# Two layers of a hybrid backbone on one core: the second FFN's input kept whole, its convolution in seven parts, and on-chip memory laid out anew

## The chip, the core and the metric

The kernel runs on one core of a Trainium2 chip. A core has five engines with queues of their own: TensorE (PE) for matrix products, VectorE (DVE), ScalarE (ACT) and GpSimd (POOL) for elementwise work, and SyncE (SP), which here only issues transfers. Transfers go over 16 DMA engines. The metric is the device time of one execution in microseconds; the median of three runs is quoted.

## The reference

Two layers, each a token mixer and a gated convolutional feed-forward network (FFN), on 1024 latent and 128 context tokens of width 1024 (`D_FF` is 2816):

```python
def _pre(x, m, g, j):
    return rmsnorm(x, g) * (1 + m[:, 3 * j + 1, None]) + m[:, 3 * j, None]

def _post(x, y, m, g, j):
    return x + m[:, 3 * j + 2, None] * rmsnorm(y, g)

def conv_ffn(h, w_up, cw, cb, w_down):
    u = dwconv(h @ w_up, cw, 1) + cb
    g, val = jnp.split(u, 2, axis=-1)
    return (jax.nn.gelu(g) * val) @ w_down

# for each layer l:
        xp = _post(xp, yp, m_p, norm_g[l, 1], 0)     # yp, ys: the mixer, with its output product @ w_out
        xs = _post(xs, ys, m_s, norm_g[l, 1], 0)
        xp = _post(xp, conv_ffn(_pre(xp, m_p, norm_g[l, 2], 1), *ffw), m_p, norm_g[l, 3], 1)
        xs = _post(xs, conv_ffn(_pre(xs, m_s, norm_g[l, 2], 1), *ffw), m_s, norm_g[l, 3], 1)
```

Layer 0's mixer is a state-space scan beside differential attention, layer 1's a short gated convolution beside a linear recurrence. All is fp32.

## The kernel before

The 1152 tokens are nine tiles of 128. Each fp32 product is made of three products of halves (`mm3`, L115): every operand is split into `hi` (a copy by ACT to a shorter fp32 format) and `lo` (the rest, a subtraction on DVE or POOL).

The stages follow one another: layer 0's mixer (to about 790 us), the first output stage (`mixer_out(0)`, L1343, to 1000), the first FFN (`ffn`, to 1840), layer 1's mixer (to 2166), the second output stage (`mixer_out(1)`, to 2267), the second FFN's up product (`up`, L1530, to 2838), its down product (`down2`, L1611, to 3139) and a tail.

**An output stage** goes over the nine tiles. For tile t, SP loads `yr` (mixer output) and `x` (residual), in layer 0 also `rb` (row scales, L1353); DVE multiplies `yr` by `rb` (L1365, layer 0 only), ACT makes `yh` (L1367), DVE `yl` (L1368), and PE runs 48 products into the tiles `ops`. `post` (ACT L289, POOL L175 and L178, DVE L303 and L304) normalizes them and adds `x`, which SP stores (L1378); `pre` (ACT L289, POOL, DVE L311) normalizes again, PE transposes (`tps`, L317), ACT applies scale and shift (`h`, L320), DVE casts (`hh`, L322) and POOL makes `hl` (L323). Both `rb` and `h` come from the pool `cv`. The order of an engine's instructions, and the slots of a pool, are set by the framework's scheduler from the program, so a tile of a pool's memory that is free late moves work in every queue.

**The second up product** forms 128 rows of both halves of `w_up` as a 2x2 block product (the 1152 tokens in two halves of `HT` = 576), with seven products in place of eight. A product (`prod`, L1489) is 24 matmuls of 128x288 into `sps`, so a block of 128 channels has 168, and there are 22 blocks (`NFB`). The input's blocks are 11, 12, 21 and 22 (512 channels by 576 tokens), and four sums of them, T1 to T4, are needed. Before, the blocks are kept as hi and lo alone; `forms` (L1500) adds them back (`whole`, L1509), makes the sums and splits these, after the first products of two blocks. Weight sums and splits are made per product (`pair`, L1478). `up_rest` (L1584) is the convolution: per half one ACT and four DVE operations over 1152 tokens, then gelu, a product and a split, and two stores of `m` per block. `down2` loads `m` back by tiles (`mt`) and the weights `wd`, and runs 1188 products `dps`.

```python
        bs = [block(fb) for fb in range(NFB)]
        next(bs[0])
        next(bs[1])
        F.extend(self.forms(H))
```

Of the kernel before, what the change touches and what calls it, by code (L numbers as in the profile page):

```python
# [39 lines left out]
class Whole:  # L40
# [9 lines left out]
class Blocks:  # L50


    def __init__(self, k):
        self.b = {x: [k.big.tile([128, 4, HT], F32R, tag="big", name=k.nm("h" + s)) for s in "hl"]
                  for x in ((0, 0), (1, 0), (1, 1), (0, 1))}

    def parts(self, q, c0, c1):
        out = []
        for n in range(2):
            a, b = max(c0, n * HT), min(c1, n * HT + HT)  # L60
            if a < b:
                out.append((a - c0, b - c0, [x[:, :, a - n * HT:b - n * HT] for x in self.b[q, n]]))
        return out
# [24 lines left out]
class K:  # L88
    def __init__(self, tc, a, o, ctx):
        self.tc, self.nc, self.a, self.o = tc, tc.nc, a, o  # L90
        self.P = lambda name, bufs, **kw: tc.tile_pool(name=name, bufs=bufs, **kw)
        self.dram = {}
        self.lastw, self.wdma = None, []
        P = lambda name, bufs, **kw: ctx.enter_context(self.P(name, bufs, **kw))
        self.dr = P("dr", 1, space=DRAM)
# [210 lines left out]
    def pre(self, t, x, tmp, cols, H):  # L306
# [5 lines left out]
        for q in range(2):  # L312
            ps = self.pt.tile([128, 4, 128], F32, tag="pt", name=self.nm("tps"))
            h = self.cv.tile([128, 4, 128], F32, tag="cv", name=self.nm("h"))
# [3 lines left out]
            for i in range(4):  # L318
                b = q * 4 + i
                nc.scalar.activation(h[:, i], ps[:, i], AF.Identity, scale=sc[:, b:b + 1], bias=sh[:, b:b + 1])  # L320
            for o0, o1, (hv, lv) in H.parts(q, t * 128, t * 128 + 128):
                nc.vector.tensor_copy(hv, h[:, :, o0:o1])  # L322
                nc.gpsimd.tensor_tensor(lv, h[:, :, o0:o1], f(hv), op=OP.subtract)  # L323
# [1019 lines left out]
    def mixer_out(self, l, W, xin, xout, H, keep={}):  # L1343
# [142 lines left out]
    def bank2(self, name):  # L1486
        return self.ps.tile([128, 2, 512], F32, tag="ps", name=self.nm(name))

    def prod(self, p, y):  # L1489

        nc = self.nc
        ps = self.bank2("sps")
        w = HT // 2
        steps = [(p[:, x, k], y[j][:, k]) for k in range(4) for x, j in ((0, 0), (0, 1), (1, 0))]
        for n, (x, y) in enumerate(steps):
            for c in range(2):
                nc.tensor.matmul(ps[:, c, :w], x, y[:, c * w:c * w + w], start=n == 0, stop=n == len(steps) - 1)  # L1497
        return ps[:, :, :w]

    def forms(self, H):  # L1500

        nc = self.nc
        V, G = nc.vector, nc.gpsimd
        T2, T1, T4 = ([self.big2.tile([128, 4, HT], F32R, tag="big2", name=self.nm(n + s)) for s in "hl"] for n in ("T2", "T1", "T4"))
        T3 = H.b[0, 1]

        def whole(out, q, n, k, eng):
            h, l = H.b[q, n]
            eng.tensor_tensor(out, f(h[:, k]), f(l[:, k]), op=OP.add)  # L1509

        def put(t, k, src, eng):
            nc.scalar.activation(t[0][:, k], src, AF.Copy)
            eng.tensor_tensor(t[1][:, k], src, f(t[0][:, k]), op=OP.subtract)
        for k in range(4):
            A, B, C = (self.mid_tile([128, 2, HT], "tf") for _ in range(3))
            whole(C[:, 0], 0, 1, k, V)
            whole(A[:, 0], 0, 0, k, G)
            whole(A[:, 1], 1, 1, k, V)
            V.tensor_tensor(A[:, 0], C[:, 0], A[:, 0], op=OP.subtract)
            V.tensor_tensor(B[:, 0], A[:, 1], A[:, 0], op=OP.subtract)  # L1520
            put(T2, k, B[:, 0], V)
            put(T1, k, A[:, 0], V)
            whole(B[:, 1], 1, 0, k, G)
            V.tensor_tensor(A[:, 1], A[:, 1], C[:, 0], op=OP.subtract)
            put(T3, k, A[:, 1], G)
            V.tensor_tensor(B[:, 1], B[:, 0], B[:, 1], op=OP.subtract)
            put(T4, k, B[:, 1], G)
        return T1, T2, T3, T4

# [389 lines left out]
```

## Time and profile before

| | |
|---|---|
| median of three runs | 3152.21 us (3146.33 to 3155.35) |
| the profiled execution | 3149.71 us, its span 3147.8 us |
| mean granted clock of PE | 0.941 |
| busy PE / DVE / POOL / ACT | 2822.0 / 2057.8 / 1250.4 / 1156.5 us |

Times in the rows below are microseconds from the start of the span. The busy share of PE is high over the whole span, so the places to read are the stages where it is not: there the chain of waits and the timeline say what PE waits for. The granted clock is given as a share of full speed.

### The profile page before, as it was taken

The numbers are of one execution on the slowest core, as the hardware profiler recorded it, in microseconds if no ns is written. First come the engines' busy times: TensorE is split into PE (matmuls) and PEld (weight loads), VectorE is DVE, ScalarE is ACT, GpSimd is POOL, SyncE is SP. The second block draws the span as 40 slices with busy tenths as digits, with TensorE's granted clock in tenths as the row PEclk, the third lists the DMA queues.
The fourth block names the chain that finished last, engine by engine and source line by source line (L and its number), as shares of the span: only waits on it lengthen the run. The fifth ranks groups of instructions, "written<-read, shape, count | busy, mean of one in ns | idle before, by whom it ended". The sixth has DMA issues, their size and how long they took to land.

```text
span 3147.8 us, 42033 instructions
## 1 busy us (share of the span) xinstructions
PE 2822.0 (90%) x15724; PEld 2536.6 (81%) x15724; DVE 2057.8 (65%) x3321; ACT 1156.5 (37%) x1946; POOL 1250.4 (40%) x1263
## 2 busy tenths in 40 slices
PE   7877888888667999999999989999879999997998
PEld 4875666777456999999999969998679999996887
DVE  6777767997323988888755686546468777773113
ACT  5221115675223322222222265555434444443101
POOL 3699954774111000000000161112467777764222
PEclk8988889998778999999999989999979999998999
DMA  6425457345222333333211232123302222229555
GB/s 212 141 82 138 109 148 200 85 106 168 88 70 72 98 91 98 89 97 97 73 41 41 67 126 76 51 84 128 121 14 101 93 93 101 93 79 249 134 105 154
DMA packets 357738, 331.46 MB, mean 105 GB/s; under 512 B 47134, under 2 KB 312050, under 8 KB 357534
## 3 DMA queue, kind: packets, MB, share of 16 engines
q1 hardware_dynamic: 273656, 264.47, 26.7%
q0 software_dynamic: 66464, 49.16, 7.3%
q10 hardware_dynamic: 17414, 15.14, 1.7%
q8 instruction: 124, 2.03, 0.3%
q14 instruction: 80, 0.66, 0.1%
HBM read 246.54 MB, written 82.16 MB: 104 GB/s over the span
## 4 chain that ended last, share of the span: by engine, by line
PE 51%; DVE 6%; POOL 5%; issue 3%; DMA 2%; ACT 2%; ACTq 0%; POOLq 0%; DVEq 0%; SPq 0%
PE pps L121 23%; PE dps L1635 8%; PE sps L1497 8%; PE dps L121 7%; PE ops L121 3%; DVE cc L1598 1%; POOL C L1536 1%; POOL ws L1536 1%; DMA wv<-ffn_w_up 1%; PE gps L121 1%; POOL wv L1536 1%; DMA mw<-w_mod 1%; ACT cc L1594 1%; POOL wp L1483 0%; DVE C L1536 0%
## 5 line engine op out<-in xcount | busy, mean ns | idle before, releaser
L121 PE MATMUL pps<-hh,whi 128*128 128x384 f32 (+1 forms) x1824 | 625.3, 343 | 1.0 <-ACT whi L131 0.5
L121 PE MATMUL pps<-hh,wlo 128*128 128x384 f32 (+1 forms) x1824 | 623.5, 342 | 2.2 <-DVE wlo L133 2.2
L121 PE MATMUL pps<-hl,whi 128*128 128x384 f32 (+1 forms) x1824 | 623.7, 342 | 0.4 <-POOL hl L831 0.4
L121 PEld LDWEIGHTS pps<-hh,whi 128*128 128x128 f32 x1824 | 349.6, 192 | 11.9 <-issue 3.2
L121 PEld LDWEIGHTS pps<-hh,wlo 128*128 128x128 f32 x1824 | 349.3, 192 | 8.4 <-DVE wlo L133 3.2
L121 PEld LDWEIGHTS pps<-hl,whi 128*128 128x128 f32 x1824 | 349.7, 192 | 4.5 <-POOL hl L831 0.7
L133 POOL TENSOR_TENSOR wlo<-wr,whi 128x1024 fp32r<-128x1024 f32 x22 | 55.1, 2510 | 740.0 <-PE dps L121 595.8
L1635 PE MATMUL dps<-wp,mt 128*128 128x512 f32 x1188 | 280.2, 398 | 20.3 <-ACT wp L1482 20.3
L1635 PEld LDWEIGHTS dps<-wp,mt 128*128 128x128 f32 x1188 | 225.2, 190 | 75.1 <-issue 20.5
L1497 PE MATMUL sps<-hh,wp 128*128 128x288 f32 x1408 | 257.5, 300 | 10.5 <-DVE wp L1483 2.5
L1497 PEld LDWEIGHTS sps<-hh,wp 128*128 128x128 f32 x1408 | 213.9, 192 | 12.8 <-issue 4.8
L1406 DVE SCALAR_TENSOR_TENSOR cc<-pps,cvc,cc 128x384 f32<-128x384 f32 (+2 forms) x352 | 171.0, 509 | 37.3 <-ACT cc L1403 35.1
L265 DVE SCALAR_TENSOR_TENSOR macc<-mw,sil,macc 128x256 f32<-128x256 f32 x392 | 175.6, 482 | 22.3 <-DMA mw<-w_mod 22.0
L1598 DVE SCALAR_TENSOR_TENSOR cc<-C,cvc,cc 128x1023 f32<-128x1023 f32 (+1 forms) x176 | 173.4, 1034 | 21.0 <-ACT cc L1594 21.0
L131 ACT ACTIVATE whi<-wr 128x1024 fp32r<-128x1024 f32 x102 | 107.6, 1057 | 164.7 <-PE pps L121 98.6
L1452 DVE TENSOR_TENSOR acc<-acc,dps 128x512 f32<-128x512 f32 x180 | 122.2, 680 | 68.8 <-PE dps L121 68.0
L1137 POOL TENSOR_TENSOR wl<-wf,wh 128x512 fp32r<-128x512 f32 (+2 forms) x96 | 144.4, 1523 | 50.6 <-DVE ra L1107 41.7
L121 PE MATMUL dps<-whi,mh 128*128 128x512 f32 x396 | 155.9, 394 | 2.3 <-DVE acc L1452 2.3
L121 PE MATMUL dps<-wlo,mh 128*128 128x512 f32 x396 | 155.3, 392 | 0.0
L121 PE MATMUL dps<-whi,ml 128*128 128x512 f32 x396 | 154.9, 391 | 0.0
L1403 ACT ACTIVATE cc<-pps,cvc 128x385 f32<-128x385 f32 (+1 forms) x132 | 87.5, 665 | 179.5 <-PE pps L121 154.0
L1497 PE MATMUL sps<-hl,wp 128*128 128x288 f32 x704 | 153.0, 299 | 0.0
(425 smaller groups left out, 6334.1 us busy)
## 6 DMA issues: line engine op xcount, KB each, us to landing
mw<-w_mod SPq DMA_DIRECT2D x224, 128.0 KB
m<-cc SPq DMA_DIRECT2D x44, 576.0 KB
x<-x SPq DMA_DIRECT2D x45, 512.0 KB
wr<-ffn_w_up SPq DMA_DIRECT2D x44, 512.0 KB
wm<-w_mod SPq DMA_DIRECT2D x40, 512.0 KB
mt<-m POOLq DMA_DIRECT2D x36, 448.0 KB, 4.7
k<-kh POOLq DMA_DIRECT2D x8, 1408.0 KB, 6.4
wr<-ffn_w_down SPq DMA_DIRECT2D x22, 512.0 KB
```

The lines of the kernel that those rows point to most:

```text
L121: nc.tensor.matmul(ps, x, y, start=first and i == 0 and j == 0, stop=last and i == n - 1 and j == 2)
L131: nc.scalar.activation(hi, raw, AF.Copy)
L133: (eng or nc.vector).tensor_tensor(lo, raw, f(hi), op=OP.subtract)
L265: nc.vector.scalar_tensor_tensor(acc[v], wt, s, acc[v], op0=OP.mult, op1=OP.add)
L1137: pin((nc.vector if late else nc.gpsimd).tensor_tensor(vl, u.wf[b][:, :k], f(vh), op=OP.subtract))
L1403: nc.scalar.activation(cc[:, :no], ps[:, q:q + no], AF.Identity, bias=cw[3], scale=cw[1])
L1406: nc.vector.scalar_tensor_tensor(cc[:, oa - o0:ob - o0], ps[:, oa + d - i0:ob + d - i0], cw[j], cc[:, oa - o0:ob - o0], op0=OP.mult, op1=O ...
L1452: nc.vector.tensor_tensor(acc[t][:, sl], acc[t][:, sl], ps, op=OP.add)
L1497: nc.tensor.matmul(ps[:, c, :w], x, y[:, c * w:c * w + w], start=n == 0, stop=n == len(steps) - 1)
L1536: tt = lambda e, o, x, y, op: e.tensor_tensor(o, x, y, op=op)
L1598: nc.vector.scalar_tensor_tensor(cc[:, o0:o1], src[:, o0 + d:o1 + d], cw[j], cc[:, o0:o1], op0=OP.mult, op1=OP.add)
L1635: nc.tensor.matmul(ps[:, h], mt[:, x, i], W[fb][:, y, h * 512:h * 512 + 512], start=i == 0 and j == 0, stop=i == n - 1 and j == 2)
```

## The change

**The input kept whole.** `Blocks` keeps the four blocks of the second FFN's input as plain fp32. T1 and T2 are formed and split in the second output stage itself, tile by tile, for the tiles of the second half (`put`). A new function `rest` splits 11, 22 and 21 and forms and splits T3 and T4; it takes 20 ACT copies, 24 DVE and 8 POOL operations of 128x576.

**The up product** is one list of products: the first product of block n+1 stands ahead of the last of block n, weights are split two products ahead, and the convolution is a generator whose seven parts stand between the next products. Its last subtraction goes from DVE to POOL; of the seven evictions DVE has five (before four), ACT two.

**Memory.** Pools wait by the tile that overlaps and not by the whole pool that was closed (`reuse_waits`); the pools of `layers` are opened in another order; `rb` has a pool of its own with one buffer; the block buffers close ahead of the last product (`early`), which then loads four weights and two tiles' rows of the down product. That product takes its first two tiles together.

```diff
@@ class Blocks: the second FFN's input
+        self.raw, self.lo, self.hi = {}, {}, {}
+        self.raw["11"] = new("r11", "b11", F32)
+        for x in ("T1", "T2"):
+            self.lo[x], self.hi[x] = new(x + "l", x + "l"), new(x + "h", x + "h")
+        for x in ("12", "22", "21"):
+            self.raw[x] = new("r" + x, "b" + x, F32)
...
+        if t * 128 + 128 > HT and q:
+            cs = slice(max(t * 128 - HT, 0), t * 128 + 128 - HT)
+            R = lambda x: self.raw[x][:, :, cs]
+            t1, t2 = (k.cv.tile([128, 4, 128], F32, tag="cv", name=k.nm("t"))[:, :, :cs.stop - cs.start] for _ in range(2))
+            V.tensor_tensor(t1, R("12"), R("11"), op=OP.subtract)
+            V.tensor_tensor(t2, R("22"), t1, op=OP.subtract)
+            for x, s, e in (("T2", t2, V), ("T1", t1, G)):
+                h, l = self.hi[x][:, :, cs], self.lo[x][:, :, cs]
+                A.activation(h, s, AF.Copy)
+                e.tensor_tensor(l, s, f(h), op=OP.subtract)
...
+        def split(x, src, e):
+            for i in range(4):
+                A.activation(self.hi[x][:, i], src[i], AF.Copy)
+                e.tensor_tensor(self.lo[x][:, i], src[i], f(self.hi[x][:, i]), op=OP.subtract)
+        raw = {x: [r[:, i] for i in range(4)] for x, r in self.raw.items()}
+        temp = lambda: [t[:, i] for t in [k.mid.tile([128, 2, HT], F32, tag="cc", bufs=4, name=k.nm("tf")) for _ in range(2)] for i in range(2)]
+        self.hi["11"], self.lo["11"] = new("h11"), new("l11")
+        split("11", raw["11"], V)
+        t3 = temp()
+        for i in range(4):
+            G.tensor_tensor(t3[i], raw["22"][i], raw["12"][i], op=OP.subtract)
+        self.hi["22"], self.lo["22"] = new("h22"), new("l22", "r12")
+        split("22", raw["22"], V)
+        t4 = temp()
+        for i in range(4):
+            V.tensor_tensor(t4[i], raw["21"][i], f(self.hi["T2"][:, i]), op=OP.subtract)
+        self.hi["21"], self.lo["21"] = new("h21", "r22"), new("l21", "r11")
+        split("21", raw["21"], G)
+        self.hi["T3"], self.lo["T3"] = new("T3h"), new("T3l")
+        split("T3", t3, V)
+        for i in range(4):
+            V.tensor_tensor(t4[i], t4[i], f(self.lo["T2"][:, i]), op=OP.subtract)
+        self.hi["T4"], self.lo["T4"] = new("T4h"), new("T4l")
+        split("T4", t4, V)
@@ K.__init__
-        self.P = lambda name, bufs, **kw: tc.tile_pool(name=name, bufs=bufs, **kw)
+        self.P = lambda name, bufs, **kw: tc.tile_pool(name=name, bufs=bufs, **({} if kw.get("space") == DRAM else {"reuse_waits": "tile"}), **kw)
@@ mixer_out
-                rb = self.cv.tile([128, 4, 128], F32, tag="cv", name=self.nm("rb"))
+                rb = self.rsb.tile([128, 4, 128], F32, tag="rb", name=self.nm("rb"))
@@ up
-        bs = [block(fb) for fb in range(NFB)]
-        next(bs[0])
-        next(bs[1])
-        F.extend(self.forms(H))
-        for fb in range(NFB):
-            next(bs[fb])
-            if fb > 0 and fb + 1 < NFB:
-                next(bs[fb + 1])
+        PRODS = (("S2", "T2", G), ("S1", "T1", V), ("11", "11", V), ("S4", "22", G), ("12", "21", V), ("S3", "T3", V), ("22", "T4", V))
+        def split(n, i):
+
+            u = fbs[n]
+            if i == 0:
+                u.s = wt("s", 1)
+                w = u.w = {"11": u.g[:, 0:4], "12": u.g[:, 4:8], "21": u.v[:, 0:4], "22": u.v[:, 4:8], "S1": u.s[:, 0:4], "S2": u.s[:, 4:8]}
+                tt(G, w["S1"], w["21"], w["22"], OP.add)
+                tt(G, w["S2"], w["S1"], w["11"], OP.subtract)
+            u.p[i] = self.pair(u.w[PRODS[i][0]], PRODS[i][2], self.wr, "p", 3)
+            if i == 1:
+                w = u.w
+                w["S4"], w["S3"] = w["S2"], w["21"]
+                tt(G, w["S4"], w["12"], w["S2"], OP.subtract)
+                tt(G, w["S3"], w["11"], w["21"], OP.subtract)
...
+        order = [(0, i) for i in range(6)]
+        for n in range(1, NFB):
+            order += [(n, 0), (n - 1, 6)] + [(n, i) for i in range(1, 6)]
+        order.append((NFB - 1, 6))
+        for u in fbs:
+            u.p, u.bank = {}, {}
+        load(0)
+        load(1)
+        split(0, 0)
+        split(0, 1)
+        rests = []
+        for m, (n, i) in enumerate(order):
+            if m + 2 < len(order):
+                split(*order[m + 2])
+            prod(n, i)
+            if m == 0:
+                H.rest(self)
+            if i == 5:
+                rests.append(self.up_rest(l, n, fbs[n].C))
+            if rests and next(rests[0], 1):
+                rests.pop(0)
+            evict(n, i)
+            if i == 6 and n + 2 < NFB:
+                load(n + 2)
+            if m == len(order) - 2:
+                early()
@@ up_rest
-        nc.vector.tensor_tensor(m, m, h, op=OP.subtract)
+        nc.gpsimd.tensor_tensor(m, m, h, op=OP.subtract)
@@ down2, layers
+            for ts in ((0, 1),) + tuple((t,) for t in range(2, NT)) if gi == 0 else tuple((t,) for t in range(NT)):
...
+            with self.P("rsb", 1) as self.rsb:
+                self.mixer_out(0, W, self.xsrc, x1, Whole(hh, hl))
...
+        def early():
+            bctx.close()
+            R = lambda name, bufs: rctx.enter_context(self.P(name, bufs, side="right"))
+            self.wrd, self.wd0, self.dm = R("wrd", 4), R("wd0", 4), R("dm", 3)
+            self.Wd = {}
+            for i in range(4):
+                self.down_w(1, i)
+                if i < 2:
+                    rows[0, i] = self.down_rows(1, 0, i)
```

The change moves instructions in every queue. Three places follow; a name ends in the program's number of the tile.

**First output stage, SP's loads and stores** (`rb`, `yr` and `x` of a tile have consecutive even numbers; the stores go to `x_7965` before and `x_7959` after). Before:

```order
L1358 DMA yr_8118<-y_5319 128x8x128
L1360 DMA x_8120<-x_sample 128x1024
L1378 DMA x_7965<-x_8014 128x1024
L1353 DMA rb_8116<-rs 128x4x128
L1358 DMA yr_8224<-y_5319 128x8x128
L1360 DMA x_8226<-x_sample 128x1024
L1378 DMA x_7965<-x_8120 128x1024
L1353 DMA rb_8222<-rs 128x4x128
```

After:

```order
L1405 DMA yr_8124<-y_5313 128x8x128
L1407 DMA x_8126<-x_sample 128x1024
L1400 DMA rb_8228<-rs 128x4x128
L1405 DMA yr_8230<-y_5313 128x8x128
L1407 DMA x_8232<-x_sample 128x1024
L1425 DMA x_7959<-x_8020 128x1024
L1400 DMA rb_8334<-rs 128x4x128
L1405 DMA yr_8336<-y_5313 128x8x128
L1407 DMA x_8338<-x_sample 128x1024
L1400 DMA rb_8440<-rs 128x4x128
```

Before, the store of tile 0 (`x_8014`) stands ahead of `rb` of tile 1 and of the loads of tile 2; now `rb`, `yr` and `x` of tile 2 stand ahead of the store of tile 0 (`x_8020`), and all loads of tile 3 with `rb` of tile 4 ahead of the store of tile 1.

**The same place on DVE**: L1365 and L1412 are the scaling by `rb`, L1368 and L1415 make `yl`, L304 and L357 add the residual, L322 and L53 cast `h`. Before:

```order
L304 SCALAR_TENSOR_TENSOR x_8014<-tmp_8071,rs,x_8014 128x1024
L311 TENSOR_SCALAR tmp_8071<-x_8014,q 128x1024
L322 CAST hh_7992<-h_8093 128x4x128
L1365 SCALAR_TENSOR_TENSOR yr_8118<-yr_8118,dag,rb_8116 128x512
L322 CAST hh_7992<-h_8105 128x4x128
L1368 TENSOR_TENSOR yl_8123<-yr_8118,yh_8122 128x1024
L303 TENSOR_TENSOR tmp_8177<-ops_8127,tab__1423_7994 128x512
L292 TENSOR_TENSOR s_8181<-ss 128x1
```

After:

```order
L1415 TENSOR_TENSOR yl_8129<-yr_8124,yh_8128 128x1024
L345 TENSOR_TENSOR s_8081<-ss 128x1
L356 TENSOR_TENSOR tmp_8077<-ops_8028,tab__1423_8000 128x512
L357 SCALAR_TENSOR_TENSOR x_8020<-tmp_8077,rs,x_8020 128x1024
L1412 SCALAR_TENSOR_TENSOR yr_8230<-yr_8230,dag,rb_8228 128x512
L364 TENSOR_SCALAR tmp_8077<-x_8020,q 128x1024
L356 TENSOR_TENSOR tmp_8183<-ops_8133,tab__1423_8000 128x512
L1415 TENSOR_TENSOR yl_8235<-yr_8230,yh_8234 128x1024
L53 CAST hh_7995<-h_8103 128x4x128
L53 CAST hh_7995<-h_8115 128x4x128
L345 TENSOR_TENSOR s_8187<-ss 128x1
```

The scaling of the next tile stood behind the cast of this tile's `h`; now the scaling of the tile after the next stands ahead of this tile's L364 and its cast.

**End of the second output stage on ACT**: `h` (before) and `b` (after) are scale and shift, `wp` the first weight pairs, L99 and L88 the copies of `rest` and `put`. Before:

```order
L289 ACTIVATE junk,ss<-ops_20254 128x512
L320 ACTIVATE h_20222<-tps_20221,mc_19408,mc_19402 128x128 x4
L320 ACTIVATE h_20234<-tps_20233,mc_19408,mc_19402 128x128 x4
L289 ACTIVATE tmp_20303,ssq<-x_20247 128x1024
L1482 ACTIVATE wp_20381<-wg_20372 128x512
L1482 ACTIVATE wp_20411<-wg_20372 128x512
L1482 ACTIVATE wp_20441<-wg_20372 128x512
L320 ACTIVATE h_20325<-tps_20324,mc_19408,mc_19402 128x128 x4
L320 ACTIVATE h_20337<-tps_20336,mc_19408,mc_19402 128x128 x4
```

After:

```order
L78 ACTIVATE b_3000_19398<-tps_20319,mc_19415,mc_19409 128x128 x4
L78 ACTIVATE b_3001_19399<-tps_20328,mc_19415,mc_19409 128x128 x4
L99 ACTIVATE h_3109_20417<-b_2995_19393 128x576 x4
L88 ACTIVATE T1h_19395<-t_20337 128x4x128
L99 ACTIVATE h_3113_20433<-b_3001_19399 128x576 x4
L88 ACTIVATE T2h_19397<-t_20338 128x4x128
L99 ACTIVATE T3h_20459<-tf_20427 128x576 x2
L99 ACTIVATE T3h_20459<-tf_20428 128x576 x2
L99 ACTIVATE h_3117_20449<-b_3002_19400 128x576 x4
L99 ACTIVATE T4h_20473<-tf_20443 128x576 x2
L99 ACTIVATE T4h_20473<-tf_20444 128x576 x2
L1522 ACTIVATE wp_20381<-ws_20378 128x512
```

Three weight pairs stood ahead of the last tile's `h`; now all copies of `rest` stand ahead of the first weight pair.

**End of the up product on SP**: `m` are the convolution's stores, `wd` and `wr` the down weights. Before:

```order
L1607 DMA m_20787<-cc_25414 128x1152
L1607 DMA m_20787<-cc_25421 128x1152
L1620 DMA wd_25689<-ffn_w_down 128x1024
L1620 DMA wd_25694<-ffn_w_down 128x1024
L1620 DMA wd_25699<-ffn_w_down 128x1024
L1620 DMA wd_25704<-ffn_w_down 128x1024
L1607 DMA m_20787<-cc_25651 128x1152
L1607 DMA m_20787<-cc_25658 128x1152
L1620 DMA wd_25709<-ffn_w_down 128x1024
```

After:

```order
L1669 DMA m_20840<-cc_25618 128x1152
L1669 DMA m_20840<-cc_25629 128x1152
L1678 DMA wr_25550<-ffn_w_down 128x1024
L1678 DMA wr_25558<-ffn_w_down 128x1024
L1678 DMA wr_25566<-ffn_w_down 128x1024
L1678 DMA wr_25571<-ffn_w_down 128x1024
L1669 DMA m_20840<-cc_25636 128x1152
L1678 DMA wr_25678<-ffn_w_down 128x1024
L1678 DMA wr_25683<-ffn_w_down 128x1024
```

The first four weights stood behind both stores of block 20 (`cc_25414`, `cc_25421`); now they stand ahead of the second of these (`cc_25636`).

## Rows read from the trace of the kernel before

**Rows 1.** The page: busy time of PE; the second down product's group.

```profile
PE 2822.0 (90%) x15724; PEld 2536.6 (81%) x15724; DVE 2057.8 (65%) x3321; ACT 1156.5 (37%) x1946; POOL 1250.4 (40%) x1263
...
L1635 PE MATMUL dps<-wp,mt 128*128 128x512 f32 x1188 | 280.2, 398 | 20.3 <-ACT wp L1482 20.3
```

**Rows 2.** Busy time, 80 us of the first output stage: PE, PEld, DVE, ACT, POOL, PEclk, DMA.

```profile
880.00:960.00 80.00, 47.68 (x176) 37.65 (x176) 21.96 (x29) 21.64 (x51) 15.44 (x20) 0.74 0.28 84
```

**Rows 3.** Timeline, one tile of the first output stage: start, length, engine, line.

```profile
851.55 0.39 PE L121 MATMUL ops<-Wo,yl 128*128 128x512 f32 x1
...
855.48 0.43 SPq L1353 DMA_DIRECT2D rb<-rs  x1
...
858.00 1.97 PE L317 MATMUL tps<-misc,tmp 128*128 128x128 f32 x8 [6.07 <-DVE tmp L311]
...
859.22 2.90 ACT L320 ACTIVATE h<-tps,mc,mc 128x128 f32<-128x128 f32 x8 [2.96 <-PE tps L317]
...
861.21 1.85 DVE L1365 SCALAR_TENSOR_TENSOR yr<-yr,dag,rb 128x512 f32<-128x512 f32 x1
...
864.26 2.07 PE L121 MATMUL ops<-wo,yh 128*128 128x512 f32 x4 [4.29 <-ACT yh L1367]
```

**Rows 4.** Busy time, a whole tile of each output stage, columns as in 2.

```profile
888.10:913.00 24.90, 14.68 (x56) 11.65 (x56) 7.20 (x10) 6.35 (x15) 5.51 (x7) 0.77 0.25 74
2197.50:2209.20 11.70, 11.70 (x57) 9.78 (x56) 5.14 (x9) 6.22 (x16) 4.14 (x6) 1.00 0.37 134
```

**Rows 5.** Chain of waits, second output stage: start, length, what.

```profile
2185.68 10.90 PE ops L121 x48
2196.59 0.87 PE tps L317 x8
...
2256.32 10.91 PE ops L121 x48
```

**Rows 6.** Timeline, last product of the first output stage's first tile.

```profile
801.75 0.39 PE L121 MATMUL ops<-Wo,yl 128*128 128x512 f32 x1
```

**Rows 7.** Chain of waits, last tile of the first output stage.

```profile
986.83 12.87 PE ops L121 x48
```

**Rows 8.** Chain of waits, from the second output stage to the first up products.

```profile
2279.32 0.51 POOL q L178
...
2285.94 18.48 PE sps L1497 x120
```

**Rows 9.** Busy time in the stall after them, columns as in 2.

```profile
2305.00:2345.00 40.00, 24.75 (x92) 19.41 (x90) 39.65 (x32) 11.71 (x19) 29.96 (x17) 0.62 0.00 0
```

**Rows 10.** Groups by line and shape, 2305 to 2353 us: times, busy, mean ns.

```profile
L1509 POOL TENSOR_TENSOR tf<-hh,hl 128x576 f32<-128x576 f32 x8 | 15.0, 1874 | 6.9 <-DVE tf L1524 6.1 <-DVE T1l L1513 0.8
L1509 DVE TENSOR_TENSOR tf<-hh,hl 128x576 f32<-128x576 f32 x8 | 11.9, 1492 | 0.0
...
L1524 DVE TENSOR_TENSOR tf<-tf,tf 128x576 f32<-128x576 f32 x4 | 3.0, 746 | 0.0
...
L1512 ACT ACTIVATE T2h<-tf 128x576 fp32r<-128x576 f32 x4 | 2.7, 680 | 2.6 <-DVE tf L1520 2.6
```

**Rows 11.** Chain of waits, steady part of the second up stage.

```profile
2566.67 22.64 PE sps L1497 x168
...
2590.18 22.64 PE sps L1497 x168
```

**Rows 12.** Timeline, from the last up products to the down product.

```profile
2835.15 2.34 SPq L1620 DMA_DIRECT2D wd<-ffn_w_down  x4
...
2835.51 1.43 POOL L1536 TENSOR_TENSOR C<-X,Y 128x576 f32<-128x576 f32 x1 [10.18 <-issue]
...
2837.61 0.42 PE L1497 MATMUL sps<-T4h,wp 128*128 128x288 f32 x2
```

**Rows 13.** Chain of waits, the same stretch.

```profile
2850.62 6.40 DMA m<-cc
...
2858.32 26.79 PE dps L1635 x102
```

More of the change, by code (lines that the diff above doesn't have):

```diff
@@ L50 @@
 class Blocks:
     def __init__(self, k):
[L54 to L58, printed above, removed]
-        for n in range(2):
[L60 to L63, printed above, removed]
+        new = lambda tag, n, dt=F32R: k.big.tile([128, 4, HT], dt, tag=tag, name=k.nm(n))
@@ new lines, in rest @@
+    def rest(self, k):
+        nc = k.nc
+        V, G, A = nc.vector, nc.gpsimd, nc.scalar
+        new = lambda n, tag=None: (k.big if tag else k.big2).tile([128, 4, HT], F32R, tag=tag or "big2", name=k.nm(n))
+        def split(x, src, e):
[18 more added lines that the diff above has]
+        split("T3", t3, V)
+        for i in range(4):
+            V.tensor_tensor(t4[i], t4[i], f(self.lo["T2"][:, i]), op=OP.subtract)
+        self.hi["T4"], self.lo["T4"] = new("T4h"), new("T4l")
+        split("T4", t4, V)
@@ L317, in pre @@
                 nc.tensor.transpose(ps[:, i], tmp[:, b * 128:(b + 1) * 128], self.id)
[L318 to L323, printed above, removed]
+            H.put(self, t, q, ps, sc, sh)
     def xsrc(self, t):
@@ L1484, in pair, with up @@
         return p
[L1486 to L1528, printed above, removed]
-    def up(self, l, H):
+    def up(self, l, H, early):
         nc = self.nc
@@ new lines, in prod, with evict @@
+        def prod(n, i):
+            u = fbs[n]
+            x = PRODS[i][1]
+            ps = u.bank[i] = self.bank2("sps")
+            y = H[x]
+            steps = [(u.p[i][:, w, k], y[j][:, k]) for k in range(4) for w, j in ((0, 0), (0, 1), (1, 0))]
+            for m, (w, z) in enumerate(steps):
+                for c in range(2):
+                    nc.tensor.matmul(ps[:, c, :W2], w, z[:, c * W2:c * W2 + W2], start=m == 0, stop=m == len(steps) - 1)
+        def evict(n, i):
+            u = fbs[n]
+            ps = u.bank[i][:, :, :W2]
+            new = lambda tag, m: self.mid.tile([128, 2, HT], F32, tag=tag, bufs=2, name=self.nm(m))
+            if i == 1:
+                X, U = new("xu", "X"), new("xu", "U")
+                u.x, u.y, u.u2, u.u3 = two(X[:, 0]), two(X[:, 1]), two(U[:, 0]), two(U[:, 1])
+                A.activation(u.y, ps, AF.Copy)
+            elif i == 2:
+                A.activation(u.x, ps, AF.Copy)
+                tt(V, u.u2, u.x, u.bank[0][:, :, :W2], OP.add)
+                u.C = [new("C", "C")]
+                u.c11, u.c12 = two(u.C[0][:, 0]), two(u.C[0][:, 1])
+                tt(G, u.c12, u.u2, u.y, OP.add)
+            elif i == 3:
+                tt(V, u.c12, u.c12, ps, OP.add)
+            elif i == 4:
+                tt(V, u.c11, u.x, ps, OP.add)
+            elif i == 5:
+                tt(V, u.u3, u.u2, ps, OP.add)
+                u.C.append(new("C", "C"))
+                tt(G, two(u.C[1][:, 1]), u.u3, u.y, OP.add)
+            elif i == 6:
+                tt(V, two(u.C[1][:, 0]), u.u3, ps, OP.add)
@@ L1584, in up_rest @@
+        for r in rests:
+            for _ in r:
+                pass
     def up_rest(self, l, fb, C):
@@ L1588, in up_rest, with row @@
         g = []
-        for s in range(2):
+        def row(s):
             b = fb + s * NFB
@@ L1624, in down2, with down_rows @@
+    def down_rows(self, l, gi, t):
+        m = self.scratch(f"m{l}", [2, NFB, 128, T])
+        fbs = self.GROUPS[gi]
+        mt = self.dm.tile([128, 2, len(fbs), 128], F32R, tag="dm", name=self.nm("mt"))
+        for x in range(2):
+            self.nc.gpsimd.dma_start(mt[:, x], m[x, fbs[0]:fbs[-1] + 1, :, t * 128:t * 128 + 128].rearrange("f p t -> p f t"))
+        return mt
+    def down2(self, l, rows, finish):
+        nc = self.nc
+        W, acc = self.Wd, []
         todo = list(range(8, NFB))
+        for fb in range(4, 8):
+            self.down_w(l, fb)
```

203 lines of the change are left out of this document (100 added, 103 removed).

## The prediction

> **What bounds the kernel now.** The page first: PE is busy for 2822 of 3147.8 us [rows 1], so what can be won without taking products away lies in the 326 us in which it is not, and in the stretches in which its clock is low. A table of busy times in 80-us slices shows where these are. One slice of the first output stage has PE at 47.7 of 80 us and a clock of 0.74 [rows 2]; the start of the second up product has 24.8 busy of 40 us at 0.62 [rows 9]; the third place is the start of the second down product, where the page's row gives a wait of 20.3 us [rows 1]. In each, the reader is to look for what ends last ahead of PE.
>
> In the first output stage that is a circle of one tile. The products of a tile end at 851.94, SP issues `rb` of the next at 855.48, the transposes start at 858.00, its eight scale-and-shift operations end at 862.12, the scaling by `rb` (L1365) of the next tile stands between the casts at 861.21, and the next products start at 864.26 [rows 3]. Nothing of tile t+1 is done while tile t is normalized. No engine is full: in 24.9 us PE works 14.7, DVE 7.2, ACT 6.4, POOL 5.5 [rows 4], and even PE's 14.7 are at a clock of 0.77. The second output stage has the same 48 products per tile, and there they stand back to back: 10.90 us of products and 0.87 of transposes, 11.77 us per tile at full clock [rows 4, 5].
>
> **The sum, part by part.** It is made against the profiled execution, 3149.71 us (its span of 3147.8 and 1.9 around it), 2.5 below the median.
>
> *First output stage.* The products of tile 0 end at 802.14, those of tile 8 at 999.70 [rows 6, 7]: 197.56 us for eight tiles, 24.7 each. In the new order SP issues `rb`, `yr` and `x` two tiles ahead, DVE scales tile t+2 before it finishes tile t, and PE has the products of t+1 ahead of the transposes of t: this is the second stage's order. What must fit into a tile is then DVE 7.2 us, ACT 6.4, POOL 5.5 [rows 4], all under 11.77; the longest circle through one tile (854 to 864) is spread over two. The two new loads that could be late are `rb`, whose single buffer is free only when the scaling has read it, and `yh`, which waits for the store of an `x`; neither has a price in these rows, since a late one has never been in PE's way. From below it costs nothing (11.77 per tile, 94.2 in all, -103.4); from above, if the scaling still waits for a load in each tile, the 3.05 us from it to the products (861.21 to 864.26 [rows 3]) are added: 14.8 per tile, -79. I take 12.1, near the lower end, since the second stage runs so: 8 x (24.7 - 12.1) = **-101**.
>
> *End of the second output stage to the first up product.* The products end at 2267.23 [rows 5]; call it E. Before, POOL had weight sums ahead of the last tile's normalization (its factor `q` is done at E+12.6), and the first `sps` start at 2285.94, E+18.7 [rows 8]. Then `forms` held PE up: of the 552.1 us to 2838.03 [rows 8, 12], 22 blocks at 22.64 [rows 11] are 498.1, so 54 are lost.
>
> Now all of `rest` stands ahead of the first weight pair. By the first stage's tile, the last raw block is ready 10.2 us after the products (851.94 to 862.12 [rows 3]). DVE then has 23 operations of some 128x576 before T4's copy can be made (3 for T1 and T2 of the last tile, 4 each for the lo of 11, of 22 and of T3 and for two rounds of T4's sum), POOL has 12 (eight of `rest`, one of T1, three weight sums). Prices: DVE 0.75 alone and 1.49 in the mean beside POOL; POOL 1.43 alone [rows 12] and 1.87 beside DVE [rows 10]. From below: 23 x 0.75 = 17.2. From above: all shared, 34.3. Between: POOL is busy for 12 x 1.87 = 22.4 us, in which DVE does 15, and the other 8 take 6 alone: 28.5. After it a copy of T4 (0.68 [rows 10]), the pair's hi (0.6, an estimate from that by its 512 columns) and its lo on POOL (1.87): 3.2. The first product starts at E + 10.2 + 28.5 + 3.2 = E+42 (bounds E+31 and E+48), not at E+18.7. I take 42, because in the stall of before DVE was full for 39.65 of 40 us beside a POOL busy for 30 [rows 9], as here.
>
> The Trainium skill ("SBUF — State Buffer", section "SBUF: two separate sides") says that an operation of DVE with two inputs in SBUF and one of GpSimd exclude each other for their whole length. By it the two queues would add up, which is rival 5. The trace agrees that each is slowed, but by less than a full exclusion: 1.87 for POOL's operation, where it and DVE's one after the other would be 2.18 [rows 10, 12].
>
> From there on PE has no more `forms`: 498.1, and 2.3 for the clock at the start (120 matmuls took 18.48 [rows 8] where 22.64/168 each would be 16.17), and 3 us in which T4's last four subtractions stand ahead of the second pair's lo on DVE. The last `sps` ends at E+545.4 = 2812.6, against 2838.03: **-25** (bounds -36 and -19 by the start alone). The gap of 0.87 us between blocks (22.64 to the next start at 23.51 [rows 11]) goes, since another product is between; if it stays, 19 come back. The moved subtraction adds 2 x 1.43 = 2.9 us to POOL's block (an estimate from the operation of half its size [rows 12]); its six operations on weights and two sums are 8 x 1.43 = 11.4 more, 14.3 of 22.64, or 18.7 with all at 1.87 [rows 10]. So it is hidden, behind the next products. If it weren't, what is late next is the lo of the next block's first pair, which stands behind it.
>
> *Start of the down product.* Weights are issued at 2835.15, the last `sps` ends at 2838.03 [rows 12], the first `dps` start at 2858.32, behind the landing of a store of `m` [rows 13]: 20.3 us. Then 102 of them take 26.79, where 280.2/1188 each would be 24.06 [rows 1, 13]: 2.7 for the clock. Now loads and splits start one product and a half earlier, about 6.5 us ahead of the last `sps`'s end (two products of 22.64/7 = 3.23), and two tiles' rows are enough for 96 products. From above: the same 21.9 us from issue (2835.15 to 2857.0) leave 15.4; if the stores of the last blocks hold them as before, 20.3. From below: two tiles less in the way, some 3. I take 9 with 1 for the clock: **-13** (0 to -18).
>
> *The rest.* The attention part has the same order, the first FFN runs on PE; the other moves of pools I put at 0 (0 to -5), since PE covers them there.
>
> Sum: 3149.71 - 101 - 25 - 13 = 3010.7; with 2.5 to the median, **3013**.
>
> **The rivals.** (1) *The first output stage keeps its period*: a load waits for a slot each tile. For it: `rb` has one buffer, and a store of `x` is in the way. Against: the loads are two tiles ahead and a tile of 24 us is longer than any of them. 3013 + 101 = 3114; a part of it (15 us per tile) 3036. (2) *`rest` gives the up product's gain back*: start at E+48, the 0.87 stays, the down product waits 20 us as before: 3013 + 6 + 19 + 13 = 3051. (3) *Slower*: POOL becomes the bound of the up product. Its block is 14.3 to 18.7 us; slower than before it would be from 22.64 + 139/22 = 29.0 us per block, that is half again above the contended price. At 30 us the time is 3013 + 22 x 7.4 = 3175. (4) *The change doesn't do what it says*: the scheduler's order is not what the chip can follow, all three places stay: 3152. (5) *DVE and POOL take turns in `rest`*: 17.2 + 12 x 1.43 = 34.4 in place of 28.5, the start at E+48, 3019. Against it: the 1.87 above.
>
> **How the numbers follow.** The forecast 0.62 with its own range 2990 to 3036; (1) whole 0.05, in part inside the range; (2) 0.13; (3) 0.03; (4) 0.02; (5) 0.08, inside the forecast's range; and 0.07 for better than 2990, where the down product starts at once and the other stages give 5. The range takes in (2) and the bounds: 2982 to 3056, with 0.13 outside. A measurement of this kernel can tell 0.3%, 9.5 us, from no change. Faster 0.95, same 0.02, slower 0.03.
>
> **What would show it.** In the first output stage, products of a tile every 12 us at clock 1.00; if the idle time of PE there ends with ACT `yh` or DVE `yr`, rival 1. First `sps` 42 us after the last `ops`, PE's wait ended by the pair of S2 on POOL; then 168 `sps` per 22.64 us with no gap. First `dps` some 9 us after the last `sps`. The prediction is wrong if the up product's blocks take over 23.5 us, or if a stage that I put at 0 has moved.

## The result, and the profile after

The changed kernel takes 3046.35 us (3041.75 to 3049.4, four runs) against 3151.94 of before: a ratio of 0.9665, interval 0.9647 to 0.9684. Forecast were 3013 and a range of 2982 to 3056. The sign is right and the time is inside the range, but 33 us above the forecast. From the first and last products of each stage in the two traces (us; the traced span is 3045.5, the sum made for it 3008.8):

| stretch | before | forecast | after |
|---|---|---|---|
| to the first `ops` of the first output stage | 790.6 | 790.6 | 789.3 |
| first output stage, first to last `ops` | 209.1 | 108 | 109.2 |
| from there to the last `ops` of the second output stage | 1267.5 | 1267.5 | 1275.6 |
| from there to the first `sps` | 18.7 | 42 | 40.5 |
| first to last `sps` | 552.1 | 503.4 | 532.4 |
| wait ahead of the first `dps` | 20.3 | 9 | 6.2 |
| first to last `dps` | 280.2 | 278.5 | 283.2 |

The page of the changed kernel, span and PE:

```profile
span 3045.5 us, 42039 instructions
...
PE 2785.9 (91%) x15724; PEld 2509.3 (82%) x15724; DVE 2123.9 (70%) x3330; ACT 1148.2 (38%) x1946; POOL 1227.1 (40%) x1218
```

Its busy time in three stretches (PE, PEld, DVE, ACT, POOL, PEclk, DMA, GB/s):

```profile
800.00:880.00 80.00, 79.63 (x374) 65.85 (x374) 43.76 (x59) 39.55 (x94) 26.48 (x39) 1.00 0.48 161
2194.00:2214.00 20.00, 0.00 (x0) 0.00 (x0) 20.00 (x20) 5.00 (x9) 12.47 (x7) 0.50 0.19 52
2400.00:2700.00 300.00, 281.25 (x2069) 275.37 (x2068) 261.25 (x235) 122.97 (x161) 221.11 (x112) 1.00 0.30 97
```

The first answers to [rows 2], in the same stage: PE is full and its clock 1.00, where it had 47.7 us at 0.74. The second lies in the stretch before the first up product: DVE is busy for all 20 us and PE for none. The third is the steady up product: PE at 281 of 300, 2069 matmuls, so a block of 168 takes 24.4 us. It was 23.5 before [rows 11].

The turning points on PE, from the timeline: last `ops`, first and last `sps`, first `dps`:

```profile
2173.74 0.40 PE L181 MATMUL ops<-Wo,yl 128*128 128x512 f32 x1
...
2214.66 0.61 PE L1585 MATMUL sps<-T2h,wp 128*128 128x288 f32 x1 [31.20 <-ACT wp L1522]
...
2746.60 0.43 PE L1585 MATMUL sps<-T4h,wp 128*128 128x288 f32 x2
2753.22 0.77 PE L1706 MATMUL dps<-wp,mt 128*128 128x512 f32 x1 [6.18 <-DMA mt<-m]
```

These answer to [rows 8, 12, 13]. The steady block of the up product, from the chain of waits (start, length, what):

```profile
2414.08 1.28 POOL wp L1523
...
2415.45 2.27 POOL ws L1532
...
2417.78 1.30 POOL ws L1532
2419.07 2.23 POOL wv L1532
...
2424.07 1.83 POOL C L1532
...
2426.59 0.75 DVE C L1532
2427.34 1.73 DVE wp L1523
2429.07 3.50 DVE cc L1659 x2
2432.57 0.67 DVE U L1532
...
2433.31 2.39 POOL C L1532
2435.71 2.64 issue
...
2438.39 1.28 POOL wp L1523
```

Before, the chain ran through 168 `sps` on end [rows 11]. Now a full turn, from 2414.08 to 2438.39, is 24.31 us and has no PE in it: POOL's lo of a pair, its weight sums, its sum `C`, DVE's evictions, a pair's lo and taps, and POOL again. What PE itself waits for in the stretch (waited for, us in total, times, longest):

```profile
PE sps L1585 <- ACT wp L1522: 31.2, 1, 31.2
PE sps L1585 <- POOL wp L1523: 24.5, 21, 1.2
```

One wait of 31.2 us at the start, then about 1.2 us in each block for a pair's lo on POOL. That lo stands in POOL's queue directly behind the moved subtraction (L1667); the third row is what DVE does meanwhile:

```profile
2425.85 2.67 POOL L1667 TENSOR_TENSOR cc<-cc,cc 128x1152 f32<-128x1152 f32 x1
2428.49 1.71 POOL L1523 TENSOR_TENSOR wp<-ws,wp 128x512 fp32r<-128x512 f32 x1
...
2427.25 1.82 DVE L1523 TENSOR_TENSOR wp<-wv,wp 128x512 fp32r<-128x512 f32 x1
```

POOL's lo, of the next block's first pair, ends at 2430.20, and PE goes on at 2430.25. This is the place that the prediction named: "If it weren't, what is late next is the lo of the next block's first pair, which stands behind it." DVE's lo takes 1.82 us, where the same operation takes 0.68 with no POOL operation beside it (2421.38), and it lies in the turn of 24.31 us above.

### The profile page after: what moved, and what is told of

It reads as the page before. It is cut to its first block, busy times and chain, and to the rows that moved or that the text cites. A ratio compares the mean times of both kernels' runs of the same rounds, so it can differ in the third digit from the quotient of the medians.

```text
span 3045.5 us, 42039 instructions
## 1 busy us (share of the span) xinstructions
PE 2785.9 (91%) x15724; PEld 2509.3 (82%) x15724; DVE 2123.9 (70%) x3330; ACT 1148.2 (38%) x1946; POOL 1227.1 (40%) x1218
## 4 chain that ended last, share of the span: by engine, by line
PE 46%; POOL 8%; DVE 8%; issue 6%; DMA 1%; ACT 1%; ACTq 0%; POOLq 0%; DVEq 0%; SPq 0%
PE pps L181 25%; PE dps L181 8%; PE dps L1706 8%; PE ops L181 3%; DVE cc L1659 3%; POOL C L1532 3%; POOL ws L1532 2%; POOL wv L1532 1%; DVE wp L1523 1%; DMA mt<-m 1%; POOL wp L1523 1%; PE gps L181 1%; DVE C L1532 1%; POOL hl L54 1%; PE sps L1585 0%
## 5 line engine op out<-in xcount | busy, mean ns | idle before, releaser
L1659 DVE SCALAR_TENSOR_TENSOR cc<-C,cvc,cc 128x1023 f32<-128x1023 f32 (+1 forms) x176 | 244.0, 1425 | 39.9 <-ACT cc L1654 39.9
L1585 PE MATMUL sps<-h,wp 128*128 128x288 f32 x1056 | 188.8, 297 | 4.5 <-DVE wp L1523 4.5
L318 DVE SCALAR_TENSOR_TENSOR macc<-mw,sil,macc 128x256 f32<-128x256 f32 x392 | 176.1, 485 | 18.7 <-DMA mw<-w_mod 17.7
L1585 PEld LDWEIGHTS sps<-h,wp 128*128 128x128 f32 x1056 | 155.9, 188 | 9.0 <-DVE wp L1523 9.0
L193 DVE TENSOR_TENSOR wlo<-wr,whi 128x1024 fp32r<-128x1024 f32 x80 | 100.4, 1256 | 53.0 <-PE pps L181 35.1
```

The source lines that it names most:

```text
L193: (eng or nc.vector).tensor_tensor(lo, raw, f(hi), op=OP.subtract)
L318: nc.vector.scalar_tensor_tensor(acc[v], wt, s, acc[v], op0=OP.mult, op1=OP.add)
L1585: nc.tensor.matmul(ps[:, c, :W2], w, z[:, c * W2:c * W2 + W2], start=m == 0, stop=m == len(steps) - 1)
L1659: nc.vector.scalar_tensor_tensor(cc[:, o0:o1], src[:, o0 + d:o1 + d], cw[j], cc[:, o0:o1], op0=OP.mult, op1=OP.add)
```

## The experiments

All times are medians; the ratio is to the kernel before, timed beside each experiment (3147.87 to 3148.53 us). Differences of a few us between two experiments are within the spread of the runs; where it matters, the stages of the traces are compared as well.

**e1, own pool for `rb` alone**, in the kernel before.

```diff
-                rb = self.cv.tile([128, 4, 128], F32, tag="cv", name=self.nm("rb"))
+                rb = self.rsb.tile([128, 4, 128], F32, tag="rb", name=self.nm("rb"))
...
+            with self.P("rsb", 1) as self.rsb:
+                self.mixer_out(0, W, self.xsrc, x1, Whole(hh, hl))
```

> The kernel before with one edit: rb gets a pool of its own with one buffer; nothing else of the change. Theory: this alone lets the loads and the scaling run two tiles ahead, so the first output stage falls from 24.7 to about 12 us per tile and the time from 3152 to about 3051. Rival: the pools' waits by tile and the new layout are needed as well, and the time stays at 3152 (24.7 us per tile).

Measured 3045.3, ratio 0.968 (0.9666 to 0.9695). 80 us of the same stage as [rows 2], 800 to 880:

```profile
800.00:880.00 80.00, 79.63 (x375) 65.82 (x374) 45.46 (x59) 40.06 (x96) 27.11 (x40) 1.00 0.47 160
```

Two edited places give as much as the whole change.

**e2, `rb` back in `cv`**, all the rest of the change kept.

```diff
-                rb = self.rsb.tile([128, 4, 128], F32, tag="rb", name=self.nm("rb"))
+                rb = self.cv.tile([128, 4, 128], F32, tag="cv", name=self.nm("rb"))
```

> The changed kernel with rb back in the pool cv. Theory: the first output stage goes back to about 24.7 us per tile and the time from 3046 to about 3147. Rival: waits by tile and layout carry the gain, and it stays at 3046.

Measured 3153.1, ratio 1.0015 (1.0005 to 1.0024). The same window:

```profile
800.00:880.00 80.00, 47.15 (x179) 37.07 (x177) 22.47 (x30) 20.97 (x49) 17.46 (x22) 0.80 0.23 75
```

So the other parts of the change sum to nothing, or a few us of loss. SP's waits show how the pool matters: the store of a tile's `x`, behind which the next tile's `rb` stands in SP's queue, waits for DVE's `x` for 163.0 us in eight times before, 161.9 in e2, but 8.0 in three times in e1.

**e3, the last subtraction on DVE again.**

```diff
-        nc.gpsimd.tensor_tensor(m, m, h, op=OP.subtract)
+        nc.vector.tensor_tensor(m, m, h, op=OP.subtract)
```

> The changed kernel with the convolution's last subtraction back on DVE (2.67 us less per block on POOL, some 1.4 more on DVE). Up blocks take 24.3 us in the changed kernel. Theory A (a circle through the queues' order sets the block, pairs stand behind convolution work): it stays at 24 or more, the time within 10 us of 3046, or gets worse, since DVE is on the circle. Theory B (POOL's added load sets the block): blocks of at most 23.5 us, the time 3028 or less.

Measured 3028.46, ratio 0.9622 (0.9608 to 0.9637): theory B. PE's wait for POOL's lo is gone (0.5 us in all for 24.5), and the up product takes 511.1 us for 532.4. 2400 to 2700 us has 2168 matmuls in place of 2069, 23.2 us per block:

```profile
2400.00:2700.00 300.00, 294.87 (x2168) 288.73 (x2166) 266.58 (x258) 128.10 (x168) 199.31 (x104) 1.00 0.28 94
```

Per block DVE is busy for 20.7 us (266.58 x 168/2168), and in the changed kernel, where it has not to subtract, for 21.2 (261.25 x 168/2069). Taking 2.5 us of work away from DVE (the mean of L1668 below) left it as full as before. Where it went shows in the groups by shape, first of the changed kernel (2400 to 2700 us; times, busy, mean ns), then of e3:

```profile
L1659 DVE SCALAR_TENSOR_TENSOR cc<-C,cvc,cc 128x1023 f32<-128x1023 f32 x49 | 88.9, 1814 | 21.5 <-ACT cc L1654 21.5
...
L1659 DVE SCALAR_TENSOR_TENSOR cc<-C,cvc,cc 128x127 f32<-128x127 f32 x49 | 55.0, 1123 | 0.0
...
L1667 POOL TENSOR_TENSOR cc<-cc,cc 128x1152 f32<-128x1152 f32 x13 | 34.9, 2682 | 0.0
```

```profile
L1660 DVE SCALAR_TENSOR_TENSOR cc<-C,cvc,cc 128x1023 f32<-128x1023 f32 x52 | 82.6, 1589 | 33.9 <-ACT cc L1655 33.9
...
L1660 DVE SCALAR_TENSOR_TENSOR cc<-C,cvc,cc 128x127 f32<-128x127 f32 x52 | 44.6, 858 | 0.0
...
L1668 DVE TENSOR_TENSOR cc<-cc,cc 128x1152 f32<-128x1152 f32 x13 | 32.3, 2483 | 0.4
```

The same taps of the convolution take 1814 and 1123 ns on the average with the subtraction on POOL, 1589 and 858 without it.

**e4, weight pairs ahead of the convolution.** `pair` keeps its last instruction on each engine in `self.lp`, and each instruction of `up_rest` is put behind it, as this one:

```diff
-            nc.scalar.activation(cc, src, AF.Identity, bias=cw[3], scale=cw[1])
+            self.behind(nc.scalar.activation(cc, src, AF.Identity, bias=cw[3], scale=cw[1]), self.lp["A"])
...
-        yield
```

> The changed kernel with each part of the convolution ordered, on its engine, behind the weight pair that the program lists ahead of it (ACT, DVE and POOL), and the generator's last empty step removed, so that seven parts take seven products. No work is added or removed. Theory A (queue order): PE no longer waits for weight pairs, blocks of about 22.7 us, the time about 3011. Theory B (load of DVE and POOL, which slow each other): blocks stay at 24 or more and the time within 10 us of 3046.

Measured 3085.29, ratio 0.98 (0.9784 to 0.9817): 39 us worse than the changed kernel, where theory B had it within 10. PE waits for pairs still, now for DVE's:

```profile
PE sps L1586 <- DVE wp L1523: 24.8, 16, 2.0
```

The wait for POOL's lo is gone (0.5 us in all), but there are also 12.0 us more for ACT's pairs and 5.4 for DVE's evictions, and a block takes 26.0 us. Theory A in this form is wrong: the order that ends one wait makes other work late. DVE is busy for 250 of 300 us here, so that it was full is not the reason.

**e8, without the last subtraction** (the lo half of `m` holds the unsplit product, so the down product adds wrong values).

```diff
-        nc.gpsimd.tensor_tensor(m, m, h, op=OP.subtract)
```

> The changed kernel without the convolution's last subtraction, on no engine (the lo half of m is left as it was, so the down product gets wrong values). If the load of POOL and DVE sets the up block, blocks fall below the 23.3 us of e3 to about 22.7 and the time to about 3012. If only the place of that instruction in POOL's queue mattered, it comes out as e3, 3028.

Measured 3013.97, ratio 0.9572 (0.9558 to 0.9587).

```profile
2400.00:2700.00 300.00, 300.00 (x2259) 300.00 (x2258) 255.79 (x258) 137.29 (x174) 180.78 (x106) 1.00 0.29 98
```

PE is full, at 22.3 us per block (the forecast had 22.64); the up product takes 493.8 us from first to last `sps`. One elementwise operation per block decides whether the block is bound by PE, and it costs on DVE too (e3 takes 14 us more than e8), so its place in POOL's queue is not all.

**e12, the subtraction on POOL in the old up product** (e1 with the reverse of e3's edit).

> e1 with one more edit: the convolution's last subtraction on POOL, in the old up product. There DVE is 74% busy and POOL 76%. If the load of POOL is what it costs, blocks rise from 23.5 to 24.5 or more and the time from 3045 by 20 us or more to about 3067. If the costs in the changed kernel came from its new order, the block stays at 23.5 and the time within 5 us of 3045.

Measured 3067.07, ratio 0.9737 (0.9719 to 0.9754), 22 above e1. The chain of waits, start of a block's weight sums and the subtraction in it:

```profile
2403.25 1.29 POOL ws L1536
...
2428.10 1.28 POOL ws L1536
...
2433.41 2.67 POOL cc L1605
...
2452.86 1.29 POOL ws L1536
```

A turn is 24.8 us (2428.10 to 2452.86; 23.4 per block in e1), and here the 2.67 us stand in the chain. The cost of the move does not hang on the new order of products, nor on a DVE that is nearly full: in e1 DVE is busy for 222 of the 300 us.

**e5 and e6, `rest` in steps.** e5 cuts it where the products need its results; e6 is that with e3's edit.

```diff
+        rs = H.rest(self)
+        next(rs)
...
-            if m == 0:
-                H.rest(self)
+            if m < 3:
+                next(rs)
```

The three later steps are 22 and T3's sum, 21 and T3, and T4, each behind the pair listed last.

> The changed kernel with rest cut into four steps: only the split of block 11 stands ahead of the first weight pairs, the split of 22 and the sum for T3 behind the pairs of the first three products, 21 and T3 one product later, T4 two products later. Theory: the first up product starts about 20 us after the second output stage's end, not 40.5, and the time falls by 12 to 18 us to about 3031, since what is left of rest then lies beside products. Rival: DVE and POOL need the same 28 us for it either way, PE waits for the splits a little later, and the time stays within 5 us of 3046.

> e5 with the convolution's last subtraction on DVE as in e3. If the two costs lie in different places (start and steady blocks) they add: 3028 less 12 to 18, about 3013. If both are the same load on DVE and POOL, it stays at 3025 or more.

e5: 3043.35, ratio 0.9669 (0.9655 to 0.9684), the rival. The first `sps` start 19.6 us after the last `ops`, 20.9 earlier, but the stretch to the last `sps` is 548.9 for 532.4. Windows of e5 where `rest` now lies:

```profile
2191.00:2211.00 20.00, 16.19 (x98) 14.58 (x98) 19.66 (x12) 9.68 (x18) 19.10 (x12) 0.92 0.09 23
2211.00:2231.00 20.00, 13.16 (x72) 12.50 (x73) 19.41 (x19) 5.48 (x10) 12.62 (x8) 0.66 0.09 27
```

DVE is at 19.7 and 19.4 of 20 us there, and PE waits for pairs that stand behind it (us in total, times, longest):

```profile
PE sps L1596 <- DVE wp L1533: 11.5, 21, 5.3
PE sps L1596 <- ACT wp L1532: 10.7, 2, 10.3
```

e6: 3021.12, ratio 0.9596 (0.9578 to 0.9614), 22 us below e5 and 7 below e3. By the stages the steps alone win 4 us (20.9 less ahead of the first `sps`, 16.5 to 16.8 more in the up product), not the 12 to 18 that were expected of them; in the medians (3 and 7) that is not clear of the spread. The subtraction costs its 21 us in the up product with or without them. e6 is the fastest version that computes all, 0.7 to 0.8% below the changed kernel.

**e11, e6 with the subtraction in halves on DVE and POOL.**

```diff
+        nc.vector.tensor_tensor(m[:, :HT], m[:, :HT], h[:, :HT], op=OP.subtract)
+        nc.gpsimd.tensor_tensor(m[:, HT:], m[:, HT:], h[:, HT:], op=OP.subtract)
```

> e6 with half of the columns of the convolution's last subtraction on each of DVE and POOL. If DVE alone set the blocks of e6 (23.3 us), the 0.7 us taken from it per block give about 10 us: 3011. If the sum of what DVE and POOL have to read sets it, POOL's 1.4 us more per block take that back: 3021 to 3030.

Measured 3030.0, ratio 0.9617 (0.9603 to 0.9631), 9 above e6, whose interval (to 0.9614) it just overlaps. In the traces the up product takes 536.4 us for 527.9, and PE waits for POOL's lo again (17.0 us in all, 0.6 in e6): what DVE is spared, POOL's share takes back and more.

**e7, e9, e10: the start of the down product.** e7 calls `early()` after everything; e9 drops `reuse_waits` from the changed kernel, e10 adds it to e1 (both with the same order on every engine).

> The changed kernel with early() called after all products and convolutions, no longer ahead of the last product. Theory: the wait ahead of the first down product goes from 6.2 us back to about 20, and the time up by 12 to 14 us to about 3059. Rival: the wait is set by the last stores, and the time stays within 5 us of 3046.

> The changed kernel without reuse_waits: a new tile again waits for whole closed pools. Every engine's instructions stand in the same order as in the changed kernel, so only waits differ. Theory: the tile waits, and not early(), took the wait ahead of the first down product from 20 to 6 us; without them it is 15 to 20 again, the time up by 9 to 14 us to about 3058. Rival: layout and order did it, and the time stays within 5 us of 3046.

> e1 (the kernel before with rb in its own pool) with reuse_waits for tiles, in the same order of instructions as e1. Theory: the wait ahead of the first down product falls from 19.1 to about 6 us and the time from 3045 to about 3032. Rival: the old layout has the weights' tiles over memory that the last convolution still uses, the wait stays at 19 and the time within 5 us of 3045.

e7: 3050.03, ratio 0.969 (0.9674 to 0.9707). e9: 3058.24, ratio 0.9713 (0.9696 to 0.973). e10: 3033.71, ratio 0.963 (0.9616 to 0.9645). PE's waits for the first down products, in e7, e9, e1 and e10:

```profile
PE dps L1705 <- DMA mt<-m: 9.0, 4, 5.5
```

```profile
PE dps L1706 <- DMA mt<-m: 7.8, 3, 6.6
```

```profile
PE dps L1635 <- ACT wp L1482: 19.1, 1, 19.1
```

```profile
PE dps L1635 <- ACT wp L1482: 12.2, 1, 12.2
```

e7 does not test its theory: the call moves in the program, the loads hardly at all. PE, DVE and POOL have the same order as in the changed kernel; on SP one store goes ahead of three weights, and on ACT two copies of weights go behind operations of the convolution. The first weights' issue on SP, in the changed kernel and in e7:

```profile
2740.68 1.76 SPq L1678 DMA_DIRECT2D wr<-ffn_w_down  x4
```

```profile
2744.49 0.33 SPq L1677 DMA_DIRECT2D wr<-ffn_w_down  x1
```

Both are 6.4 us ahead of the end of the last `sps` (2747.03 and 2750.84); before it was 2.9 us [rows 12]. In e9 the issue is as early and the wait stays as well, so tile waits did not take it away: that theory falls, though e9's time is the one that was expected. Its 12 us are spread (3.8 at the first stage's start, 2.4 in the up product, 3.9 in the down product), and the first and the last vary as much between other runs (starts of 786.0 to 796.1 us, down products of 279.3 to 286.6), so one trace doesn't tell why. In the old layout waits by tile take 7 of the 19 us away. There ACT copies the first down weight 11.1 us behind the last `sps`, in the changed kernel 2.8 ahead of its end. In all runs, the kernels with the new up product issue weights 6.1 to 6.4 us ahead and wait 4.7 to 9.5; those with the old one issue them 0.6 to 2.9 ahead and wait 12.2 to 21.7. No run takes the early issue alone away.

## Why the prediction was right, and what its sum missed

**First output stage, right.** -101 was forecast and -100 measured, 12 us per tile at full clock. e1 and e2 show the cause from both sides: the pool that `rb` shared. The prediction put it on the new order as such, which is how the pool acts (e2), and did not single out the pool. This one stage is 100 of the 106 us that were won; it carries the forecast.

**Start of the up product, right.** E+42 was forecast, E+40.5 measured, DVE full as expected. One term was not needed: PE started with the hi that ACT makes of the first pair (the wait of 31.2 us ends there), not behind its lo on POOL, put at 1.87 us.

**The up product itself, the step that failed.** The forecast had blocks at PE's 22.64 us, and of the moved subtraction it said: "So it is hidden, behind the next products." It costs 21 to 24 us of the up product (e3; e6 against e5; e12 against e1) and about as much of the whole time (18 to 22 by the medians, 14 to 23 by the ratios), and without it PE is full (e8). The step added up POOL's own time, 14.3 to 18.7 of 22.64, and took an engine with time left as cover. But POOL's queue has an order, and PE waits for the lo behind the subtraction, as the prediction itself named it; and the operation also stretches what DVE does meanwhile. How much of the cost is the one and how much the other is not separated. The gap between blocks, which was to go ("if it stays, 19 come back"), stays as this wait: 24.5 us in all. 29 us of the miss are here (532.4 for 503.4). Rival 3 looked at POOL and put it at 29 us per block to be slower than before; the block came at 24.4, with POOL busy for 221 of 300 us, so POOL as such is not the bound. Rival 2's outcome, that the up product gives nothing, is what happened, by another path: 18.7 + 552.1 before, 40.5 + 532.4 after. The range had room for that rival, at 3051, and so for this miss.

**Down product, right in size and, as far as shown, in cause.** Weights were to be issued about 6.5 us ahead of the last `sps`'s end and were so 6.4 ahead; the wait is 6.2 us for 9. The products themselves take 283.2 us for 278.5, so that -11 is measured for -13. What in the change makes the issue early is not shown, since e7 leaves it where it was.

**What was put at 0** moved by 8.1 us between the two output stages: 3.3 in the first FFN, 2.5 in layer 1's mixer, 2.4 in the second output stage. The kernels with the new input blocks and layout all have 1274.5 to 1277.8 us there, those with the old (before, e1, e10, e12) 1266.9 to 1268.1. So it comes with the blocks or the layout, not with waits by tile, which e10 has and e9 has not. PE's waits there don't show more, and it stays open.

The prediction named two signs that it would be wrong: blocks of over 23.5 us, or a moved stage that was put at 0. Both came. What was right is the first output stage, the start and the down product; the up product's term was not.

## What to carry to other kernels

A small buffer that shares a pool with later work can hold back a whole stage: before a rewrite, look at which pool the first late load comes from. Idle time of POOL is no free room, even with DVE busy for 74% of the stage (e1, e12); price an operation moved there by what it adds to DVE's operations and by what stands behind it in POOL's queue, not by POOL's share. In this stage, moving work to another place in time (e5) won little and putting part of it first (e4) lost. An experiment that moves a call needs a look at whether the instructions moved with it (e7).

## What the runs showed of the hardware

Short operations suffer most beside POOL. From the changed kernel's timeline, a tap of 1023 columns and one of 127 with POOL idle or waiting:

```profile
2433.16 1.27 DVE L1659 SCALAR_TENSOR_TENSOR cc<-C,cvc,cc 128x1023 f32<-128x1023 f32 x1
...
2436.18 0.34 DVE L1659 SCALAR_TENSOR_TENSOR cc<-C,cvc,cc 128x127 f32<-128x127 f32 x1
```

and four taps (two of each) with three operations of POOL among them:

```profile
2415.27 6.19 DVE L1659 SCALAR_TENSOR_TENSOR cc<-C,cvc,cc 128x1023 f32<-128x1023 f32 x4 [1.79 <-ACT cc L1654]
...
2415.45 2.25 POOL L1532 TENSOR_TENSOR ws<-wv 128x512 f32<-128x512 f32 x1
...
2417.78 1.30 POOL L1532 TENSOR_TENSOR ws<-ws,wg 128x512 f32<-128x512 f32 x1
...
2419.03 2.27 POOL L1532 TENSOR_TENSOR wv<-wg,wv 128x512 f32<-128x512 f32 x1
```

Alone the four are 3.2 us (2 x 1.27 + 2 x 0.34); they took 6.19, in which POOL finished three operations of about 1.3 us each alone. One after the other all would be 7.1, so DVE and POOL take turns, with some 0.15 us of overlap at each turn (an estimate: 0.9 us over six turns). Of the 49 taps of 127 columns in 2400 to 2700 us, the 12 with no POOL operation beside them take 0.34 us and the other 37 take 1.37 to 1.39: each of these pays for nearly a whole operation of POOL. In e3 they are 26 and 26, which makes the lower mean. DVE's 63 sums with a tile of `sps`, which lies in PSUM, the memory that PE writes, take 0.74 to 0.76 us with POOL or without; the taps and the lo operations, with both inputs in SBUF, the engines' own memory, are the ones that are stretched.

The prediction read POOL's mean of 1.87 us [rows 10] as less than an exclusion. The eight operations take 1.80 to 1.98 us each, where one after the other with DVE's would be 2.18: turns again, with the same overlap, which is why adding both queues up (rival 5, E+48) came out too late. The rule of the Trainium skill ("SBUF — State Buffer", section "Who interferes with whom") is that one of the two holds the shared port pair for its whole instruction and the other is blocked. The trace agrees with the turns, but not quite with the whole instruction, by the overlap.
